# Two-layer trunk on one core: where the end of the first layer splits conv weights, and where the residual is formed

## The chip, the cores and the metric

The kernel runs on one core of a Trainium2 chip: TensorE (matmuls and transposes; in profiles PE, its weight loads PEld), VectorE (DVE), ScalarE (ACT), GpSimd (POOL) and SyncE (SP, which only issues DMAs here). The metric is the device time of one execution in microseconds (us). One run of the profiler gives a trace of one execution; times in it count from its first instruction.

## The reference, cut to what matters

Two layers over 512 latent tokens of width 1024 (the first also reads 256 context tokens). Each layer is a mixer, a post-norm, a mixture of 16 experts and a second post-norm. The change lies where the first layer ends and the second layer's mixer begins.

```python
def _post_norm(h, branch, g, b):
    return _layer_norm(DEEPNORM_ALPHA * h + branch, g, b)

def _short_conv_mixer(u, w_in, conv_w, w_out):              # second layer
    b_gate, c_gate, x_in = jnp.split(u @ w_in, 3, axis=-1)
    z = lax.conv_general_dilated(c_gate * x_in, conv_w[:, None, :], ...)   # depthwise, width 3
    return (b_gate * z) @ w_out

    # in each layer
    u_lat = _modulate(h_lat, m_lat[0], m_lat[1])            # h * (1 + scale) + shift
    y_lat = ...mixer(u_lat, ...)
    h_lat = _post_norm(h_lat, m_lat[2] * y_lat, ln_mix_g[layer], ln_mix_b[layer])
    f_lat = _expert_choice_ffn(_modulate(h_lat, m_lat[3], m_lat[4]), ...)
    h_lat = _post_norm(h_lat, m_lat[5] * f_lat, ln_ffn_g[layer], ln_ffn_b[layer])
```

All data is fp32. Where fp32 accuracy of a projection is needed, both operands are split into a high part (rounded to fp32r) and a low part (the rest), and three matmuls hh + hl + lh are summed.

## The kernel before

**Data.** `A` and `H` are two tiles of 128 x 4 x 1024 (token tile `t` of 4, then the features). In the experts `A` collects the sum of the residual and the experts' outputs, and `H` holds the normed tokens without gain and bias. Gain and bias go into the modulation of the next projection (`NG`) and, separately, into the residual of the next post-norm: alpha * (n * gain + bias).

**The end of the first layer** (`moe`, last expert, e = 15). TensorE transposes the last hidden state (L1380), builds the scatter matrix (L1322), and then makes four rows of 512 that hold the residual's gain and bias on all partitions (`ln_row`: L283 on TensorE, L285 on ScalarE, 16 fp32 matmuls, which the trace shows as 32 passes). Behind them come the last down projection in two column halves (`out_mm`, L1412, from the transfers `wdl`), the scattered sums (L1428) and the norms: for token tiles 0 and 1 VectorE takes the statistics (L1448), the inverse root (L261, L262 on ScalarE; L268 to L273 on VectorE) and writes `H` (L1544).

**Weights of the input projection.** `wci` comes in eight pieces `ci0` to `ci7`, one per block of 128 columns; each holds three sets (C, x and B gate), so set `i` = 3f + b belongs to block f. `prep_conv(i)` splits set `i`: a cast on ScalarE (L247, 128x1024) and a subtraction on GpSimd or VectorE (L248), into one of four slots of a ring. Before the change sets 0 to 2 are split in `open_conv`, ahead of the norms in program order, and set 3 behind the second norm; all four subtractions run on GpSimd.

**The residual** (`residual`, L293 and L294): for each half of a token tile GpSimd multiplies `H` by the gain row and adds the bias row, 128x512 each, into `A`: 16 instructions, eight behind the first two norms and eight behind the last two.

**Then** `post1` makes the projection's input: for each half b of the tokens and each group g of two feature blocks TensorE transposes (L1584), ScalarE modulates (L1588) and casts (L247), VectorE subtracts (L248). `conv_in` is the projection's matmuls (L252 to L254) into `p_c`: the first block's three sums in the banks g, u and d (`p_c_g`, `p_c_u`, `p_c_d`), first for tokens 0 to 255, then for 256 to 511.

**The mixer's loop** (`layer1_mixer`) runs over f = 0 to 7 and b = 0 to 2. Each step is one `conv_in`, the split of set i + 3 (GpSimd; for i = 1 VectorE), one step of the modulation of this layer, and the gate, convolution and product for the block: L1660 on ScalarE, L1662, L1663, L1665 and L1668 on VectorE, then the split of the result for the output projection. The modulation's weights (`wmod`, pieces m1_4 to m1_11) are not multiplied on TensorE: VectorE sums them (L347, L349, eight per piece) into `rows`, and TensorE only adds over the partitions (L407 or L313), at a fixed place in its queue between two blocks. In the last two blocks GpSimd takes a part of these sums (L363, L365).

**What sets the order.** The program order is written out by hand; each engine runs its own instructions in that order and waits at each for what it needs. SP issues the transfers in one queue: a piece of weights is issued when the block that it goes to has been read (`next_load`). So m1_4 goes out when the three sets of `ci0` have been split.

Of the kernel before, what the change touches and what calls it, by code (L numbers as in the profile page):

```python
# [8 lines left out]
F32 = mybir.dt.float32  # L9
F32R = mybir.dt.float32r  # L10
BF16 = mybir.dt.bfloat16
AF = mybir.ActivationFunctionType
ALU = mybir.AluOpType
# [177 lines left out]
class Trunk:  # L191
# [1065 lines left out]
    def moe(self, layer):  # L1257
# [6 lines left out]
        with tc.tile_pool(name=f"ex{layer}", bufs=2) as wk:  # L1264
# [87 lines left out]
            for e in range(NE):  # L1352
                xe = xes[e // 2]
                before = prev

                def scatters(t0):
                    for t in (t0, t0 + 1) if before else ():
                        scatter(*before, t)

                p_g = product("g", lambda k: xe[k // KH][:, k % KH, e % 2], f"g{layer}_{e}", (lambda: scatters(0) if e == NE - 1 else None) if e else lambda: gather(0, 4, KO), e == 0)  # L1360
                sg = wk.tile([P, 512], F32, name="sg", bufs=1)
                nc.scalar.activation(sg, p_g, AF.Silu)
                if e == NE - 1:
                    scatters(2)
                g = e // 2 + 1
                if g < NE // 2 and e % 2 == 0:
                    sel_build(g)
                p_u = product("u", lambda k: xe[k // KH][:, k % KH, e % 2], f"u{layer}_{e}", None, e == 0)
                if e == 0 and self.late:
                    self.late()  # L1370
                hid = self.rows()
                nc.vector.tensor_tensor(hid, sg, p_u, ALU.mult)  # L1372

                if e < NE - 1:
                    scatters(0)
                if g < NE // 2:
                    gather(g, 4 * (e % 2), 4 * (e % 2) + 4, tag="g")
                p_t = self.bank("tr", (P, 4, P), "p_t")
                for q in range(4):
                    nc.tensor.transpose(p_t[:, q], hid[:, q * P:(q + 1) * P], self.cv("ident"))  # L1380
                hT = wk.tile([P, 4, P], F32, name="hT", bufs=1)
                nc.vector.tensor_copy(hT, p_t)
                if e < NE - 1:
                    scatters(2)
                st = scatter_sel(e)
                if self.spare and not gb:
                    gb += [self.spare[:, v * D:v * D + D] for v in range(2)]
                    g1 = [side(v) for v in gb]
                    for v in range(2):
                        self.ln_row(4 * layer + 2 + v, g1[v], 1.0 if last else ALPHA)  # L1390
                lhs = lambda k: hT[:, k % 4, (k // 4) * CAP:(k // 4) * CAP + CAP]
                yp = wk.tile([P, 2, 512], F32R, name="yp", bufs=1)
                if e < NE - 1:
                    split_y(product("d", lhs, f"d{layer}_{e}"), yp, self.m5b)
                    prev = (e, st, yp)
# [81 lines left out]
            for t in range(TT):  # L1477
                if t < 2 - last:
                    part(t, 0)
                else:  # L1480
                    early_sum(t, 0)
            out_mm(1, KH, KO)
            for t in range(2 - last, TT):
                if last:
# [55 lines left out]
            else:  # L1540
# [9 lines left out]
                for t in range(2):  # L1550
                    newton[t]()
                    norm(t)
                self.rs.append(self.prep_conv(3, nc.gpsimd))
                for t in (2, 3):
                    nc.vector.bn_stats(bst[:, t, 0], A[:, t, 0:512])
                total(2)
# [2 lines left out]
                total(3)  # L1559
                for g in range(2, 4):  # L1560
                    self.post1(0, g, wk)
                for t in range(2):
                    self.residual(t, g1)
                rstd(2, 4)()
                for t in (2, 3):
                    norm(t)
# [1 line left out]
                self.p_c = [self.bank(q, name="p_c") for q in "gud"]  # L1568
                self.conv_in(self.p_c[0], self.rs[0], 0, 256)
                self.conv_in(self.p_c[1], self.rs[1], 0, 256)  # L1570
                for g in range(4):
                    self.post1(1, g, wk)
                for t in range(2, TT):
                    self.residual(t, g1)

    def post1(self, b, g, wk):

# [15 lines left out]
    def conv_in(self, out, r, n0, n1):  # L1593
        uH, uL = self.u1
        for k in range(KO):
            self.mm3(out[:, n0:n1], r[:, 0, k], r[:, 1, k], uH[:, k, n0:n1], uL[:, k, n0:n1], k == 0, k == KO - 1)

    def open_conv(self):

        self.rblk, self.ublk = self.freed[-4:-2], self.freed[-2:]  # L1600
        self.ring = [self.block(b, F32R).rearrange("p (i s k c) -> p i s k c", i=2, s=2, k=KO) for b in self.rblk]
        self.rs = [self.prep_conv(i, self.nc.gpsimd) for i in range(3)]
        self.next_load(self.w["ci0"][1])
        self.u1 = [self.block(b, F32R).rearrange("p (k n) -> p k n", k=KO) for b in self.ublk]

    def prep_conv(self, i, eng=None):
# [6 lines left out]
    def layer1_mixer(self):  # L1613
        nc, tc, ins, base = self.nc, self.tc, self.ins, self.base
        uH, uL = self.u1
        with tc.tile_pool(name="l1", bufs=1) as pool:
# [1 line left out]
            gL = pool.tile([P, KO, S], F32R, name="gL")  # L1618
            rx, ry = self.rblk

            hx = base.tile([P, TT, D], F32, tag="H", name="H")
            self.H = hx
            self.load_gates(1, hx[:, 3])
            cbs, zbs = ([hx[:, a, i * 512:i * 512 + 512] for i in range(2)] for a in range(2))
            tb = hx[:, 2, 0:S + 2]
# [16 lines left out]
            for f in range(KO):  # L1642
# [4 lines left out]
                for b in range(3):  # L1647
                    i = 3 * f + b
                    p_b = self.bank(name=f"p_c{b}") if f else p_c[b]
                    self.conv_in(p_b, rs[i], 0 if f else 256, 512)  # L1650
                    if i and i + 3 < 3 * KO:
                        rs.append(self.prep_conv(i + 3, nc.gpsimd if i > 1 else None))
                    elif i + 3 >= 3 * KO:

                        out_rows(i - 1)
# [53 lines left out]
```

## Time and profile before

| | before |
|---|---|
| median of 3 runs | 1477.01 us (1476.96 to 1478.04) |
| the profiled execution | 1474.1 us |
| its span, first to last instruction | 1472.0 us |
| TensorE matmuls, busy | 1370.1 us (93%) |
| VectorE | 708.2 us (48%) |
| ScalarE | 335.9 us (23%) |
| GpSimd | 269.7 us (18%) |

Read it by stages: the first layer's experts run to about 737 us, the norms and the first matmuls of the second layer from there to 790, its input projection to about 924, and the second layer's experts start near 1000. Busy shares over the whole span say little on the stretch from 737 to 924, where the change lies. A row of the timeline gives start, length, engine, line, operation, output<-input, shape, and how often it ran in a row; in brackets stand the engine's idle time before it and what ended that.

### The profile page before, as it was taken

The numbers are of one execution on the slowest core, as the hardware profiler recorded it, in microseconds if no ns is written. First come the engines' busy times: TensorE is split into PE (matmuls) and PEld (weight loads), VectorE is DVE, ScalarE is ACT, GpSimd is POOL, SyncE is SP. The second block draws the span as 40 slices with busy tenths as digits, with TensorE's granted clock in tenths as the row PEclk, the third lists the DMA queues.
The fourth block names the chain that finished last, engine by engine and source line by source line (L and its number), as shares of the span: only waits on it lengthen the run. The fifth ranks groups of instructions, "written<-read, shape, count | busy, mean of one in ns | idle before, by whom it ended". The sixth has DMA issues, their size and how long they took to land. (4 is left out here: it accounts for less than half of the span.)

```text
span 1472.0 us, 17439 instructions
## 1 busy us (share of the span) xinstructions
PE 1370.1 (93%) x7162; PEld 775.1 (53%) x7162; DVE 708.2 (48%) x1158; ACT 335.9 (23%) x661; POOL 269.7 (18%) x239
## 2 busy tenths in 40 slices
PE   7989988889999999999959999989999999999993
PEld 4865546754454444443348787775444454454342
DVE  3684768823243343332476798660333334243246
ACT  2455661321111111011043222231101111111113
POOL 1321628550000000000065445005000000000003
PEclk9989999789999999999979999989999999999996
DMA  9337337789999999999962554749999999999991
GB/s 373 157 130 288 134 136 314 297 322 394 427 426 427 427 427 426 427 426 427 417 277 78 230 229 172 276 180 350 423 427 427 426 426 427 426 427 427 426 407 65
DMA packets 42527, 490.35 MB, mean 333 GB/s; under 512 B 4752, under 2 KB 5200, under 8 KB 13136
## 3 DMA queue, kind: packets, MB, share of 16 engines
q1 hardware_dynamic: 41856, 486.10, 80.1%
q10 hardware_dynamic: 592, 3.15, 0.6%
q8 instruction: 56, 0.92, 0.2%
q14 instruction: 23, 0.19, 0.0%
HBM read 487.13 MB, written 2.10 MB: 332 GB/s over the span
## 5 line engine op out<-in xcount | busy, mean ns | idle before, releaser
L1312 PE MATMUL p_u<-blk,xe 128*64 128x512 f32 x1024 | 226.2, 593 | 6.2 <-DMA blk<-wu 6.2
L1312 PE MATMUL p_g<-blk,xe 128*64 128x512 f32 x1024 | 226.2, 593 | 2.2 <-ACT xe L1299 2.2
L1312 PE MATMUL p_d<-blk,hT 128*64 128x512 f32 x960 | 212.6, 595 | 0.0
L1372 DVE TENSOR_TENSOR rows<-sg,p_u 128x512 f32<-128x512 f32 x32 | 22.0, 688 | 326.1 <-PE p_u L1312 316.0
L1343 DVE SCALAR_TENSOR_TENSOR A<-p_sc_sc,gates,A 128x512 f32<-128x512 f32 x240 | 163.1, 742 | 6.0 <-PE p_sc_sc L1340 6.0
L1312 PEld LDWEIGHTS p_u<-blk,xe 128*64 128x64 f32 x1024 | 72.5, 137 | 154.2 <-issue 140.6
L1312 PEld LDWEIGHTS p_g<-blk,xe 128*64 128x64 f32 x1024 | 72.6, 137 | 146.9 <-issue 139.7
L1402 POOL COPY m5c<-m5b 64x256 f32<-64x256 f32 x8 | 3.2, 394 | 721.9 <-PE p_ga_g L1290 721.6
L1312 PEld LDWEIGHTS p_d<-blk,hT 128*64 128x64 f32 x960 | 66.0, 137 | 129.3 <-issue 129.2
L1299 ACT ACTIVATE xe<-p_ga_g,FG 128x128 f32<-128x128 f32 x112 | 42.1, 455 | 306.5 <-PE p_ga_g L1290 306.5
L1290 PEld LDWEIGHTS p_ga_g<-sel,H 128*128 128x128 f32 x896 | 104.2, 192 | 3.1 <-issue 0.8
L1290 PE MATMUL p_ga_g<-sel,H 128*128 128x128 f32 x896 | 104.7, 275 | 0.0
L1334 ACT CAST yp<-rows 64x512 fp32r<-64x512 f32 (+1 forms) x68 | 40.2, 591 | 270.5 <-DVE rows L1331 269.6
L1331 DVE TENSOR_TENSOR rows<-p_d,m5b 128x512 f32<-128x512 f32 x30 | 20.8, 692 | 134.4 <-PE p_d L1312 134.4
L1340 PE MATMUL p_sc_sc<-yp,st 128*128 128x512 f32 x240 | 72.8, 421 | 1.0 <-DVE A L1343 1.0
L248 POOL TENSOR_TENSOR blk<-blk,blk 128x1024 fp32r<-128x1024 f32 (+1 forms) x25 | 59.8, 2412 | 66.4 <-ACT blk L247 66.4
L252 PE MATMUL p_c_sc<-blk,blk 128*128 128x512 f32 x168 | 67.3, 401 | 0.0
L253 PE MATMUL p_c_sc<-blk,blk 128*128 128x512 f32 x168 | 65.9, 392 | 0.0
L254 PE MATMUL p_c_sc<-blk,blk 128*128 128x512 f32 x168 | 65.8, 392 | 0.0
L1340 PEld LDWEIGHTS p_sc_sc<-yp,st 128*128 128x128 f32 x240 | 40.6, 188 | 34.3 <-issue 24.3
L1335 DVE TENSOR_TENSOR yp<-rows,yp 64x512 fp32r<-64x512 f32 (+1 forms) x68 | 45.6, 671 | 25.3 <-ACT yp L1334 24.2
L349 DVE SCALAR_TENSOR_TENSOR rows<-blk,cond,rows 128x512 f32<-128x512 f32 x49 | 54.2, 1106 | 1.5
(397 smaller groups left out, 2007.7 us busy)
## 6 DMA issues: line engine op xcount, KB each, us to landing
blk<-wg SPq DMA_DIRECT2D x60, 2048.0 KB, 27.8
blk<-wu SPq DMA_DIRECT2D x60, 2048.0 KB, 22.0
blk<-wd SPq DMA_DIRECT2D x56, 2048.0 KB, 26.1
blk<-wmod SPq DMA_DIRECT2D x23, 2048.0 KB, 8.7
blk<-wci SPq DMA_DIRECT2D x8, 1536.0 KB, 12.1
blk<-wd SPq DMA_DIRECT2D x8, 1024.0 KB, 6.7
blk<-wg SPq DMA_DIRECT2D x8, 1024.0 KB, 9.4
blk<-wu SPq DMA_DIRECT2D x16, 512.0 KB, 22.9
```

The lines of the kernel that those rows point to most:

```text
L248: (eng or nc.vector).tensor_tensor(lo, src, hi.bitcast(F32), ALU.subtract)
L252: mm(out, ah, bh, start=start, stop=False)
L253: mm(out, ah, bl, start=False, stop=False)
L254: mm(out, al, bh, start=False, stop=stop)
L349: nc.vector.scalar_tensor_tensor(a, W[:, k], c, a, ALU.mult, ALU.add)
L1290: nc.tensor.matmul(pg[:, j - j0], H[:, t, j * P:(j + 1) * P], sels[g][:, t, e0:e1].rearrange("p e s -> p (e s)"), start=t == 0, stop=t == ...
L1299: nc.scalar.activation(o, pg[:, j - j0], AF.Identity, bias=self.FG[:, 1, j:j + 1], scale=self.FG[:, 0, j:j + 1])
L1312: nc.tensor.matmul(o[64 * hf:64 * hf + 64], lhs(k), W[:, kk, hf * 512:hf * 512 + 512], start=k == 0, stop=k == KO - 1)
L1334: nc.scalar.copy(yp[r, hf], ye[r])
L1335: nc.vector.tensor_tensor(yp[q, hf], ye[r], yp[r, hf].bitcast(F32), ALU.subtract)
L1340: nc.tensor.matmul(pp[hf], st[:, t * P:(t + 1) * P], yp[:, hf], start=True, stop=True)
L1343: nc.vector.scalar_tensor_tensor(a, pp[hf], self.gateT[:, t, e:e + 1], a, ALU.mult, ALU.add)
```

## The change

- The first layer's `ln_row` calls are gone from the last expert. They stand in the mixer's loop at i = 1 (gain) and i = 2 (bias), into tiles of their own (`l1gb`).
- `open_ring` splits set 0 between the two halves of the last down projection's second column half (cast and subtraction on ScalarE and GpSimd). `open_conv` splits set 1 on GpSimd. Set 2 is split by VectorE behind the last norm, and `next_load` of `ci0`'s block stands behind it. Set 3 is split on GpSimd between the groups of the second half's `post1`.
- The residual is formed in place in the tile of the normed tokens, in the mixer's loop at i = 4, 6, ..., 18: one half of a token tile each time (one multiplication, one addition on GpSimd). The mixer's scratch `hx` takes the other tile; the two names `A` and `H` change places.

```diff
@@ moe
-                if self.spare and not gb:
+                if last and self.spare and not gb:
                     gb += [self.spare[:, v * D:v * D + D] for v in range(2)]
                     g1 = [side(v) for v in gb]
                     for v in range(2):
-                        self.ln_row(4 * layer + 2 + v, g1[v], 1.0 if last else ALPHA)
+                        self.ln_row(4 * layer + 2 + v, g1[v], 1.0)
@@ moe, behind the first half of out_mm(1) and the sums of column half 0
+            if not last:
+                self.open_ring()
             out_mm(1, KH, KO)
@@ moe, behind the norms of tiles 0 and 1
-                self.rs.append(self.prep_conv(3, nc.gpsimd))
...
-                for t in range(2):
-                    self.residual(t, g1)
                 rstd(2, 4)()
                 for t in (2, 3):
                     norm(t)
...
                 self.conv_in(self.p_c[0], self.rs[0], 0, 256)
                 self.conv_in(self.p_c[1], self.rs[1], 0, 256)
+                self.rs.append(self.prep_conv(2))
+                self.next_load(self.w["ci0"][1])
                 for g in range(4):
                     self.post1(1, g, wk)
-                for t in range(2, TT):
-                    self.residual(t, g1)
+                    if g == 1:
+                        self.rs.append(self.prep_conv(3, nc.gpsimd))
@@
+    def open_ring(self):
+
+        self.rblk = self.freed[-3:-1]
+        self.ring = [self.block(b, F32R).rearrange("p (i s k c) -> p i s k c", i=2, s=2, k=KO) for b in self.rblk]
+        self.rs = [self.prep_conv(0, self.nc.gpsimd)]
+
     def open_conv(self):
-
-        self.rblk, self.ublk = self.freed[-4:-2], self.freed[-2:]
-        self.ring = [...]
-        self.rs = [self.prep_conv(i, self.nc.gpsimd) for i in range(3)]
-        self.next_load(self.w["ci0"][1])
+        assert self.rblk == self.freed[-4:-2]
+        self.ublk = self.freed[-2:]
+        self.rs.append(self.prep_conv(1, self.nc.gpsimd))
@@ layer1_mixer
-            hx = base.tile([P, TT, D], F32, tag="H", name="H")
-            self.H = hx
+            hx = base.tile([P, TT, D], F32, tag="A", name="A")
+            self.H, self.A = hx, self.H
+            gb = [[pool.tile([P, 512], F32, name=f"l1gb{v}{h}") for h in range(2)] for v in range(2)]
+
+            def residual(q):
+                a = self.A[:, q // 2, (q % 2) * 512:(q % 2) * 512 + 512]
+                nc.gpsimd.tensor_tensor(a, a, gb[0][q % 2], ALU.mult)
+                nc.gpsimd.tensor_tensor(a, a, gb[1][q % 2], ALU.add)
+
...
                     self.conv_in(p_b, rs[i], 0 if f else 256, 512)
+                    if i in (1, 2):
+                        self.ln_row(1 + i, gb[i - 1], ALPHA)
+                    if i in range(4, 20, 2):
+                        residual(i // 2 - 2)
                     if i and i + 3 < 3 * KO:
                         rs.append(self.prep_conv(i + 3, nc.gpsimd if i > 1 else None))
```

What stands in the engines' queues, first TensorE at the end of the last expert, before (-) against now (`p_gb` are the gain and bias rows, `p_d` and `p_u` the two column halves of the down projection):

```order
 L1322 LDWEIGHTS identb
 L1322 MATMUL p_sb_tr<-slotb,identb 128x512
-L283 MATMUL p_gb_sc<-lnr,cst 128x128 x16
 L1412 MATMUL p_d<-blk_124_4248,hT 64x256 x16
 L1412 MATMUL p_u<-blk_125_4261,hT 64x256 x8
```

The 16 matmuls of the rows no longer stand ahead of the down projection. Next GpSimd from the early sums (L1423) on, before (`blk_126` is `ci0`, `blk_127` is `ci1`, `blk_130` the gain and bias rows):

```order
L1423 TENSOR_TENSOR A<-A,l_y 128x512 x2
L248 TENSOR_TENSOR blk_131_4531<-blk_126_4277,blk_131_4531 128x1024 x2
L248 TENSOR_TENSOR blk_132_4532<-blk_126_4277,blk_132_4532 128x1024
L248 TENSOR_TENSOR blk_132_4532<-blk_127_4287,blk_132_4532 128x1024
L293 TENSOR_TENSOR A<-H,blk_130_4414 128x512
L294 TENSOR_TENSOR A<-A,blk_130_4414 128x512
```

and now (L1632 and L1633 are the residual, `l1gb` its rows; `blk_128` is `ci2`):

```order
L1423 TENSOR_TENSOR A<-A,l_y 128x512 x2
L248 TENSOR_TENSOR blk_131_4493<-blk_126_4277,blk_131_4493 128x1024 x2
L248 TENSOR_TENSOR blk_132_4494<-blk_127_4287,blk_132_4494 128x1024
L1638 MEMSET A 128x1
L1639 MEMSET A 128x1
L248 TENSOR_TENSOR blk_131_4493<-blk_127_4287,blk_131_4493 128x1024
L248 TENSOR_TENSOR blk_132_4494<-blk_128_4336,blk_132_4494 128x1024
L1632 TENSOR_TENSOR H<-H,l1gb_4717 128x512
L1633 TENSOR_TENSOR H<-H,l1gb_4719 128x512
```

Sets 0 and 1 stand directly behind the early sums, set 3 behind them, and the first pair of the residual behind the splits of sets 5 and 6; before, the residual's eight pairs stood between set 3 and set 5. Last ScalarE at the start of the mixer's loop, before:

```order
L1660 COPY H<-p_c_g 128x512
L247 CAST blk_131_4531<-blk_127_4287 128x1024 x2
L247 CAST gH<-H 128x512
L247 CAST blk_132_4532<-blk_128_4336 128x1024
L1660 COPY H<-p_c_sc 128x512
```

and now:

```order
L1676 COPY A<-p_c_g 128x512
L285 ACTIVATE l1gb_4717<-p_gb_sc 128x512
L285 ACTIVATE l1gb_4718<-p_gb_sc 128x512
L247 CAST blk_131_4493<-blk_127_4287 128x1024
L285 ACTIVATE l1gb_4719<-p_gb_sc 128x512
L285 ACTIVATE l1gb_4720<-p_gb_sc 128x512
L247 CAST blk_131_4493<-blk_127_4287 128x1024
L247 CAST gH<-A 128x512
```

Two copies of the gain rows stand ahead of the cast of set 4, and two of the bias rows ahead of that of set 5.

## Rows read from the trace of the kernel before

**Rows 1.** Windows: busy us (count) of PE, PEld, DVE, ACT, POOL; clock; DMA.
```profile
753.00:766.00 13.00, 1.34 (x5) 1.05 (x6) 12.62 (x19) 2.61 (x6) 12.29 (x7) 0.53 0.59 231
840.00:908.00 68.00, 68.00 (x312) 56.34 (x310) 62.04 (x62) 15.73 (x19) 37.57 (x17) 1.00 0.56 222
```
**Rows 2.** Timeline of TensorE at the last expert's end: start, us, what, [idle before].
```profile
737.00 3.83 PE L283 MATMUL p_gb_sc<-lnr,cst 64*128 64x128 f32 x32
740.77 3.67 PE L1412 MATMUL p_d<-blk,hT 128*64 128x256 f32 x32
...
747.46 1.95 PE L1412 MATMUL p_u<-blk,hT 128*64 128x256 f32 x16
```
**Rows 3.** SP's issues there, and us from issue to landing (last number).
```profile
723.92 9.24 SPq L215 DMA_DIRECT2D blk<-wdl  x8
...
734.16 0.33 SPq L215 DMA_DIRECT2D blk<-wci  x1
...
blk<-wdl SPq DMA_DIRECT2D x1, 512.0 KB, 10.2
...
blk<-wci SPq DMA_DIRECT2D x1, 1536.0 KB, 12.6
```
**Rows 4.** Timeline of ScalarE: the cast of the second column half.
```profile
750.07 0.83 ACT L1334 CAST yp<-rows 64x256 fp32r<-64x256 f32 x2 [1.47 <-DVE rows L1331]
```
**Rows 5.** Timeline of GpSimd and VectorE around the norms.
```profile
752.05 9.25 POOL L248 TENSOR_TENSOR blk<-blk,blk 128x1024 fp32r<-128x1024 f32 x4 [1.40 <-ACT blk L247]
...
755.63 1.09 DVE L268 SCALAR_TENSOR_TENSOR rs_t<-l_r 128x1 f32<-128x1 f32 x1
...
761.77 0.21 DVE L268 SCALAR_TENSOR_TENSOR rs_t<-l_r 128x1 f32<-128x1 f32 x1
...
763.24 1.84 DVE L1544 TENSOR_SCALAR H<-A,l_nm,l_r 128x1024 f32<-128x1024 f32 x1
...
775.38 1.54 DVE L1544 TENSOR_SCALAR H<-A,l_nm,l_r 128x1024 f32<-128x1024 f32 x2
```
**Rows 6.** Timeline of VectorE: the subtractions of the projection's input.
```profile
768.24 2.79 DVE L248 TENSOR_TENSOR blk<-u1t,blk 128x512 fp32r<-128x512 f32 x2
...
782.25 6.65 DVE L248 TENSOR_TENSOR blk<-u1t,blk 128x512 fp32r<-128x512 f32 x4 [5.34 <-ACT blk L247]
```
**Rows 7.** Timeline of ScalarE and VectorE at the start of the mixer's loop.
```profile
789.85 0.59 ACT L1660 COPY H<-p_c_g 128x512 f32<-128x512 f32 x1 [2.92 <-PE p_c_g L254]
790.33 1.05 ACT L247 CAST blk<-blk 128x1024 fp32r<-128x1024 f32 x1
792.61 1.05 ACT L247 CAST blk<-blk 128x1024 fp32r<-128x1024 f32 x1 [1.23 <-PE p_c_u L253]
...
791.47 1.23 DVE L248 TENSOR_TENSOR blk<-blk,blk 128x1024 fp32r<-128x1024 f32 x1 [2.57 <-ACT blk L247]
...
807.37 0.69 DVE L409 TENSOR_TENSOR H<-mod_b_sc,H 128x512 f32<-128x512 f32 x1 [1.94 <-PE mod_b_sc L407]
```
**Rows 8.** Timeline of VectorE without and with GpSimd beside it; then that window.
```profile
850.71 1.54 DVE L1665 SCALAR_TENSOR_TENSOR H<-H,vec 128x512 f32<-128x512 f32 x2
852.16 3.11 DVE L349 SCALAR_TENSOR_TENSOR rows<-blk,cond,rows 128x512 f32<-128x512 f32 x4
...
900.89 2.85 DVE L1665 SCALAR_TENSOR_TENSOR H<-H,vec 128x512 f32<-128x512 f32 x2
903.67 6.37 DVE L349 SCALAR_TENSOR_TENSOR rows<-blk,cond,rows 128x512 f32<-128x512 f32 x4
...
901.76:909.96 8.20, 6.31 (x28) 4.88 (x26) 8.06 (x6) 0.00 (x0) 7.97 (x6) 1.00 0.00 0
```
**Rows 9.** Timeline of VectorE: what it waits for in the projection.
```profile
829.03 1.57 DVE L347 TENSOR_SCALAR rows<-blk,cond 128x512 f32<-128x512 f32 x1 [6.19 <-DMA blk<-wmod]
...
874.35 0.16 DVE L318 TENSOR_TENSOR mlat<-mod_pc_sc,vec 128x4 f32<-128x4 f32 x1 [1.10 <-PE mod_pc_sc L313]
...
891.62 0.16 DVE L318 TENSOR_TENSOR mlat<-mod_pc_sc,vec 128x4 f32<-128x4 f32 x1 [1.46 <-PE mod_pc_sc L313]
```

More of the change, by code (lines that the diff above doesn't have):

```diff
@@ L1596, in conv_in @@
             self.mm3(out[:, n0:n1], r[:, 0, k], r[:, 1, k], uH[:, k, n0:n1], uL[:, k, n0:n1], k == 0, k == KO - 1)
+    def open_ring(self):
+        self.rblk = self.freed[-3:-1]
+        self.ring = [self.block(b, F32R).rearrange("p (i s k c) -> p i s k c", i=2, s=2, k=KO) for b in self.rblk]
+        self.rs = [self.prep_conv(0, self.nc.gpsimd)]
     def open_conv(self):
-        self.rblk, self.ublk = self.freed[-4:-2], self.freed[-2:]
-        self.ring = [self.block(b, F32R).rearrange("p (i s k c) -> p i s k c", i=2, s=2, k=KO) for b in self.rblk]
-        self.rs = [self.prep_conv(i, self.nc.gpsimd) for i in range(3)]
-        self.next_load(self.w["ci0"][1])
+        assert self.rblk == self.freed[-4:-2]
+        self.ublk = self.freed[-2:]
+        self.rs.append(self.prep_conv(1, self.nc.gpsimd))
         self.u1 = [self.block(b, F32R).rearrange("p (k n) -> p k n", k=KO) for b in self.ublk]
```

## The prediction

> **What bounds the kernel now.** I read the windows by stage first. Between 753 and 766 us TensorE works 1.34 us of 13 at a granted clock of 0.53, while VectorE and GpSimd are both busy for over 12 us; between 840 and 908 us TensorE is busy all 68 us, VectorE 62 and GpSimd 37.6 [rows 1]. So the change touches two stages with different limits. At the end of the first layer TensorE waits for VectorE's norms. In the input projection of the second layer TensorE is the bound, but with VectorE right behind it. Next I read the waits there: between 840 and 908 us VectorE waits for TensorE only twice, 1.10 and 1.46 us, and before that once for a weight transfer, 6.19 us [rows 9]. That is all the room it has for delay.
>
> The third view is the timeline of VectorE beside that of GpSimd, and it gives the price on which everything turns. Six VectorE instructions (two L1665, four L349) take 1.54 + 3.11 = 4.65 us when GpSimd stands still. The same six took 2.85 + 6.37 = 9.22 us beside GpSimd's short multiplies and adds: six of those and six of VectorE's share the window from 901.76 to 909.96, GpSimd busy for 7.97 us of it [rows 8]. That is 0.76 us lost for each GpSimd instruction: the two engines take turns, each waiting for the other's instruction to end. The second price comes from the residual itself: four L248 took 6.65 us beside four of its instructions [rows 6], against 4 x 0.78 = 3.11 at the pace of the free L349, so 0.88 us each.
>
> **Part by part, on the way to the end of p_c_g (the first block of the input projection).**
> 1. The four rows of gain and bias leave TensorE's queue ahead of the last expert's output. L283 took 3.83 us from 737.00 and L1412 began at 740.77 without a wait [rows 2]. Its weights are there earlier: eight parts were issued from 723.92 on, and each lands 10.2 us later, the first at 734.1, the last (issued 8.9 us after it) at 743.0 [rows 3]. The matmuls that read the last two began at 747.46 [rows 2], now at 743.7, and come to the last part near 744.6. So the whole is won: **-3.8**.
> 2. ScalarE's cast for ring block 0 now stands ahead of the second L1334. It waits for ci0, issued at 734.16 and landed 12.6 us later, at 746.8 [rows 3], and takes 1.05 us [rows 7], to 747.8. L1334 began at 750.07 [rows 4] and could begin at 746.3. So **+1.5**.
> 3. VectorE's stretch from 755.63 to the end of the second norm at 765.08 took 9.45 us while GpSimd split four sets from 752.05 to 761.30 without a break [rows 5]. Free of that it holds two norms (1.54) and six tiny instructions, of which the unhindered one took 0.21 [rows 5]: about 2.8 us. GpSimd's two early splits (9.25 / 4 = 2.3 us each) run from 747.8 to 752.5, and the stretch now begins near 753.4, so they are over: **-6.7**.
> 4. The first two L248 took 2.79 us beside the residual [rows 6], against 1.56 free: **-1.2**. The next two gain less, since ScalarE's pace feeds them; I count them as nothing.
> 5. In the second half the four L248 lose their neighbours too, but ScalarE gets a further cast (1.05 us) between them and sets the pace: **-0.5**, bounds 0 and -1.5. Split 2 on VectorE stands beside TensorE's projection of p_c_g and p_c_u, which hides it; the transfer that it releases (m1_4, next in SP's queue) is issued some 9 us later than before, and is needed only at VectorE's first L347, behind the split of step 6.
> Together -10.7 at the end of p_c_g: ScalarE's copy moves from 789.85 [rows 7] to about 779.1. TensorE's granted clock was 0.53 between 753 and 766 us [rows 1], nearly all at the lower of its two levels (1.2 GHz), after it had waited for the norms; I keep that. If it stayed at 2.4 GHz, some 4 us of matmuls there would take half: 2 us more won (an estimate), as bound.
>
> **In the input projection.**
> 6. ScalarE's cast for ring block 4 began at 790.33, half a us after the copy, and VectorE's split of it at 791.47 [rows 7]. Now two copies of the gain stand ahead of it on ScalarE, and those wait for half of L283, which waits for p_c_u (done at 792.61, 2.8 us after the copy began). So 2.8 + 1.9 + 0.6 (a copy of that size, row 789.85) puts the cast at 784.4 and VectorE's split at 785.6: of 10.7 us, 5.9 are left on VectorE. TensorE pays all of L283 again, 3.8 us, in a stretch that has no idle time; the bias matmul that VectorE's L409 waited for (807.37, after a wait of 1.94 [rows 7]) comes 10.7 - 3.8 = 6.9 us earlier, and VectorE is there by then. **Won at that place: 6.9 us.** With nothing else the change would end there: 1467.2 in the profiled execution.
> 7. The residual: 16 GpSimd instructions of 128x512 between the splits of column blocks 1 to 6. Before, they stood in the stage of the norms (part of what steps 3 to 5 win back); now they stand beside VectorE's sums and convolution, which have two operands in SBUF. I take 0.88, since it is the price of these very instructions: 16 x 0.88 = 14.1 us. From it go the two waits for TensorE (1.10 + 1.46) and about 0.9 for an instruction of residual 2 that runs inside the wait of 6.19 us: 10.6 us on VectorE. TensorE's bias and column matmuls (L407, L313) wait for VectorE's sums in its own queue, so each us that VectorE falls behind stops TensorE. **+10.6.** Lower bound: VectorE is idle 6 of the 68 us [rows 1], and L1662 and L1668 read PSUM; about an eighth of the instructions would fall beside those, so 0.76 x 7/8 = 0.66, or 10.6 - 3.5 = 7.1. Upper bound: VectorE loses the whole of each instruction, 1.33 us (7.97 / 6 [rows 8]): 21.3 - 3.5 = 17.8.
>
> What the rows show of this (0.76 and 0.88 lost for instructions of about 1.3 us) bears on a rule of the Trainium skill, "SBUF — State Buffer", section "Who interferes with whom": a VectorE instruction with two SBUF inputs contends with a GpSimd instruction that reads SBUF, and the one that starts first holds the shared ports for its whole length. By the rule the loss may be the whole 1.33 us each, which would give +10.9 instead of +3.7, and 1487.9; the rows lie below it because VectorE often asks when part of the GpSimd instruction is already over.
>
> **Sum.** -6.9 + 10.6 = +3.7 us. The profiled execution took 1474.1 us (span 1472.0); the median of the runs is 1477.01, 2.9 above it. So 1477.8 in a profiled execution and 1480.7 as a median. Behind the projection every weight load is released by the projection's own instructions, so I let the shift through to the end unchanged.
>
> **Rivals.**
> A. *The residual hides.* GpSimd stood idle for 30 of the 68 us between 840 and 908 [rows 1]; if its short instructions met only VectorE instructions that read PSUM or wait, the 6.9 us would stay: 1470.1. It decides at a price of (6.9 + 3.5) / 16 = 0.65 us for even, and of 0.46 for a gain of 0.2%. Against it: VectorE's 62 of 68 us [rows 1] and both measured prices. Half of the residuals stand ahead of a split whose cast is done, not in the idle stretch.
> B. *Even.* VectorE's price comes out near 0.65, because the splits behind the residual move into stretches in which VectorE waits: 1474.1 to 1479.9, say 1477.
> C. *The early splits still run beside the norms.* If ci0 or ScalarE's two casts come 2 us later than I count, split 1 (2.3 us) blocks L268 as it did at 755.63 (1.09 us [rows 5]) and TensorE idles on: 3.7 + 2.3, or 1483.0. That is the case in which the change does not do what it says.
>
> **How the numbers follow.** A difference of under 0.2% (2.95 us) can't be told from no change here. Forecast 0.60, and a sixth of it lies within 0.2%; A 0.13; B 0.20; C 0.07. Faster: A and a tenth of B, 0.15. Same: 0.10 of the forecast and 0.18 of B, 0.28. Slower: 0.50 + 0.07 = 0.57. Range: the sum runs from -6.9 + 7.1 = +0.2 to +10.9, and the clock adds 2 at the lower end: 1475 to 1488. The upper end needs the worst price for all sixteen, so I stop at 1486.5, which with A leaves out under 2 in 10.
>
> **What would show it.** Step 1: L1412 directly behind L1322, near 737.0. Step 2: ScalarE idle until 746.8 ahead of the first L247. Step 3: the second norm ends near 756 us, none of the six tiny instructions over 0.3 us. Steps 4 and 5: the copy L1676 near 779. Step 6: VectorE idle for over 5 us ahead of a split that begins near 785.6. Step 7: L1681 and L349 of 1.4 to 1.8 us beside L1632 and L1633, and TensorE waits ahead of L407 and L313 that sum to some 7 to 10 us more than before. I am wrong if TensorE is as dense between 800 and 900 us as before; then the price of the residual is what failed. If the copy of step 5 stands at 783 or later, the early gain failed.

## The result, and the profile after

The changed kernel takes 1484.78 us (median of 4 runs, 1483.59 to 1485.99) against 1476.99 before: ratio 1.0056, 95% interval 1.0040 to 1.0072; by the medians it is 7.8 us slower. The prediction was 1480.7, 3.7 slower: the right side, inside its range, and half the size. Its profiled execution took 1485.99 us.

Executions start the stretch at slightly different times, so traces are compared here from L1322, the scatter matrix ahead of the last down projection: 736.70 before, 735.58 after. "Earlier" and "later" below are counted from it.

TensorE's timeline after (start, us, what, [idle before]):

```profile
735.58 0.38 PE L1322 MATMUL p_sb_tr<-slotb,identb 128*128 128x512 bf16 x1 [0.78 <-DVE hT L1382]
735.88 3.67 PE L1412 MATMUL p_d<-blk,hT 128*64 128x256 f32 x32
...
749.61 0.55 PE L1428 MATMUL p_sc_sc<-yp,st 128*128 128x256 f32 x1 [5.10 <-DVE yp L1335]
752.00 1.44 PE L1428 MATMUL p_sc_sc<-yp,st 128*128 128x256 f32 x5 [1.84 <-DVE yp L1335]
757.88 0.48 PE L1585 MATMUL p_tr_sc<-cst,H 128*128 128x128 f32 x1 [4.45 <-DVE H L1546]
...
934.08 0.50 PE L252 MATMUL p_y_sc<-blk,gH 128*128 128x512 f32 x1
```

L1412 stands directly behind L1322: the rows are gone from there. But TensorE now waits 5.10 and 1.84 us for the split of the hidden rows (L1335), where before it was 1.68; its first wait for the norms is 4.45 us instead of 9.62. The last line is the first matmul of the output projection, p_y; before:

```profile
736.70 0.38 PE L1322 MATMUL p_sb_tr<-slotb,identb 128*128 128x512 bf16 x1 [0.78 <-DVE hT L1382]
...
751.08 1.21 PE L1428 MATMUL p_sc_sc<-yp,st 128*128 128x256 f32 x6 [1.68 <-DVE yp L1335]
761.91 0.47 PE L1584 MATMUL p_tr_sc<-cst,H 128*128 128x128 f32 x1 [9.62 <-DVE H L1544]
...
924.85 0.50 PE L252 MATMUL p_y_sc<-blk,gH 128*128 128x512 f32 x1
```

From L1322 to p_y it is 188.15 us before and 198.50 after: 10.4 later. VectorE and GpSimd after, the two timelines behind those first waits:

```profile
747.10 4.85 DVE L1335 TENSOR_TENSOR yp<-rows,yp 64x256 fp32r<-64x256 f32 x2 [1.95 <-ACT yp L1334]
...
758.38 0.81 DVE L1546 TENSOR_SCALAR H<-A,l_nm,l_r 128x1024 f32<-128x1024 f32 x1
...
746.83 4.83 POOL L248 TENSOR_TENSOR blk<-blk,blk 128x1024 fp32r<-128x1024 f32 x2 [1.08 <-ACT blk L247]
```

The two early splits run from 746.83 to 751.66, and two small subtractions of VectorE, which take 0.87 us without a neighbour (the first line of e3 below), end 0.3 us behind them. The second norm (758.38) is done 4.8 us earlier than in [rows 5], not 9. ScalarE and VectorE after, at the start of the loop:

```profile
780.63 0.58 ACT L1676 COPY A<-p_c_g 128x512 f32<-128x512 f32 x1 [1.68 <-PE p_c_g L254]
784.59 0.60 ACT L285 ACTIVATE l1gb<-p_gb_sc 128x512 f32<-128x512 f32 x1 [3.38 <-PE p_gb_sc L283]
785.48 0.60 ACT L285 ACTIVATE l1gb<-p_gb_sc 128x512 f32<-128x512 f32 x1 [0.30 <-PE p_gb_sc L283]
785.98 1.04 ACT L247 CAST blk<-blk 128x1024 fp32r<-128x1024 f32 x1
...
787.05 1.22 DVE L248 TENSOR_TENSOR blk<-blk,blk 128x1024 fp32r<-128x1024 f32 x1 [7.37 <-ACT blk L247]
```

The copy of p_c_g is 8.1 us earlier than in [rows 7], the split of set 4 only 3.3, after a wait of 7.37 us. From there VectorE falls behind. TensorE's waits in the loop (in all, times, longest), before:

```profile
PE mod_b_sc L412 <- DVE rows L349: 2.1, 1, 2.1
PE mod_b_sc L407 <- DVE rows L349: 2.1, 1, 2.1
PE mod_pc_sc L313 <- DVE rows L349: 0.9, 1, 0.9
```

and after:

```profile
PE mod_b_sc L407 <- DVE rows L349: 6.2, 1, 6.2
PE mod_b_sc L412 <- DVE rows L349: 5.0, 1, 5.0
PE mod_pc_sc L313 <- DVE rows L349: 4.9, 3, 2.3
```

The windows from the first bias matmul (m4) to p_y (columns as in [rows 1]), before, with the stretch behind the wait of 2.07 us under it:

```profile
806.31:924.85 118.54, 113.42 (x498) 90.77 (x496) 100.75 (x111) 26.81 (x36) 55.55 (x28) 0.99 0.53 210
820.32:838.74 18.42, 17.48 (x74) 13.82 (x75) 11.22 (x16) 4.06 (x5) 7.15 (x3) 1.00 0.58 229
```

and after, with the stretch behind the wait of 6.15 us:

```profile
801.48:934.08 132.60, 116.56 (x497) 92.00 (x495) 117.90 (x111) 26.93 (x37) 81.83 (x44) 0.95 0.48 190
819.57:824.00 4.43, 4.43 (x8) 2.82 (x9) 1.93 (x3) 2.99 (x4) 2.21 (x1) 0.50 0.86 281
```

That stage grew by 14.06 us. 10.92 of it is idle time of TensorE (16.04 against 5.12). The other 3.14 is TensorE's own time for the same matmuls: the granted clock over the stage fell from 0.99 to 0.95. Directly behind the wait of 6.15 us it is 0.50, the lower level (1.2 GHz), for 4.43 us; behind the wait of 2.07 us before it was 1.00.

### The profile page after: what moved, and what is told of

Read it like the earlier page. It is cut to its first block, busy times and chain, and to the rows that moved or that the text cites. A ratio compares the mean times of both kernels' runs of the same rounds, so it can differ in the third digit from the quotient of the medians.

```text
span 1484.1 us, 17438 instructions
## 1 busy us (share of the span) xinstructions
PE 1375.2 (93%) x7162; PEld 777.5 (52%) x7162; DVE 718.7 (48%) x1159; ACT 335.7 (23%) x661; POOL 270.7 (18%) x238
## 4 chain that ended last, share of the span: by engine, by line
PE 62%; DMA 17%; DVE 16%; ACT 2%; issue 2%; DVEq 0%; SPq 0%; ACTq 0%
PE p_g L1312 11%; PE p_d L1312 11%; PE p_u L1312 10%; DMA blk<-wg 5%; DMA blk<-wu 5%; DMA blk<-wd 5%; PE p_ga_g L1290 5%; DVE rows L349 3%; PE p_sc_sc L1340 3%; PE p_y_sc L252 2%; PE p_y_sc L254 2%; PE p_y_sc L253 2%; DVE A L1681 1%; PE mod_R L306 1%; PE p_o L931 1%
## 5 line engine op out<-in xcount | busy, mean ns | idle before, releaser
L1334 ACT CAST yp<-rows 64x512 fp32r<-64x512 f32 (+1 forms) x68 | 40.2, 591 | 279.3 <-DVE rows L1331 278.5
L1343 DVE SCALAR_TENSOR_TENSOR A<-p_sc_sc,gates,A 128x512 f32<-128x512 f32 x120 | 81.6, 743 | 3.0 <-PE p_sc_sc L1340 3.0
L1343 DVE SCALAR_TENSOR_TENSOR H<-p_sc_sc,gates,H 128x512 f32<-128x512 f32 x120 | 81.6, 743 | 3.0 <-PE p_sc_sc L1340 3.0
L248 POOL TENSOR_TENSOR blk<-blk,blk 128x1024 fp32r<-128x1024 f32 (+1 forms) x24 | 59.4, 2487 | 79.8 <-ACT blk L247 79.8
L1335 DVE TENSOR_TENSOR yp<-rows,yp 64x512 fp32r<-64x512 f32 (+1 forms) x68 | 49.6, 730 | 27.0 <-ACT yp L1334 26.0
L349 DVE SCALAR_TENSOR_TENSOR rows<-blk,cond,rows 128x512 f32<-128x512 f32 x49 | 61.5, 1255 | 1.5
L1362 ACT ACTIVATE sg<-p_g 128x512 f32<-128x512 f32 x32 | 19.1, 597 | 154.3 <-PE p_g L1312 154.3
```

The lines of the kernel that those rows point to most:

```text
L248: (eng or nc.vector).tensor_tensor(lo, src, hi.bitcast(F32), ALU.subtract)
L349: nc.vector.scalar_tensor_tensor(a, W[:, k], c, a, ALU.mult, ALU.add)
L1334: nc.scalar.copy(yp[r, hf], ye[r])
L1335: nc.vector.tensor_tensor(yp[q, hf], ye[r], yp[r, hf].bitcast(F32), ALU.subtract)
L1343: nc.vector.scalar_tensor_tensor(a, pp[hf], self.gateT[:, t, e:e + 1], a, ALU.mult, ALU.add)
```

## The experiments

Ratios are to the kernel before, run beside it on the same chip; differences in us between runs are worked out from them, unless a median is named. Each interval reaches 2 to 3 us to either side, so a difference of that size between two runs rests on the traces. "At p_y" is the place of p_y in the trace, counted from L1322, against before. Sums of VectorE's durations in the expectations count the small overlap of neighbours; the windows shown here don't, and read some 3 us less.

### The changed kernel again (e9)

> The changed kernel once more, unaltered, beside the two others of this call: a second trace of it and more runs. Ratio to before 1.004 to 1.0072 if the first comparison holds. The first trace lay 10.4 us behind the one of before at the first matmul of the output projection, while the medians differ by 7.8; if the first trace is typical, this one shows 9.5 to 11 at the same place, counted from the scatter matrix of the last expert (L1322).

Ratio 1.0054 (1.0035 to 1.0073); at p_y 11.3 us later, just above what was expected. So both traces lie 10.4 to 11.3 behind, and both comparisons of medians give 7.7 to 7.8. The loop repeats (m4 to p_y 132.70 us, against 132.60 in the first trace); the copy of p_c_g is 7.2 us earlier than before, against 8.1. The executions differ from one another where nothing was changed, too: L1322 stands anywhere from 734.3 to 737.7 us in the traces of this study. What makes up the 3 us between traces and medians was not found; the kernel before has one trace only, of an execution 2.9 us below its median.

### The residual left out (e1)

```diff
-                    if i in range(4, 20, 2):
-                        residual(i // 2 - 2)
```

> The 16 instructions of the residual on GpSimd are left out (what the second layer's post-norm adds is then the normed tile without gain and bias); their rows are still made. In the changed kernel VectorE's instructions between its split of set 4 and the bias matmul of m10 took 45.6 us longer than the shortest of their kind, in the kernel before 27.4. Only 13.2 of the 45.6 stand beside the residual itself; the splits' share grew too, 22.5 to 27.2. Theory 1 (the residual is the cause, both by its own turns and by pushing the splits into stretches where VectorE is dense): the excess falls to 25 to 30 us, TensorE's waits ahead of the bias and column matmuls from 16 us to about 5, and the time to 1471 to 1475 (ratio to before 0.996 to 0.9985). Theory 2 (only the 13.2 us of direct turns matter): excess near 32, time 1475 to 1479. Rival (the rows in the mixer's loop and the late start of set 4's cast set the time): above 1481.

Ratio 0.9966 (0.9952 to 0.9980): 5 us faster than before, 13 less than the changed kernel; at p_y 3.1 us earlier. The windows from the copy of p_c_g to the bias matmul of m10, after and then e1:

```profile
780.63:918.96 138.33, 122.30 (x572) 100.15 (x571) 118.68 (x108) 29.06 (x37) 84.45 (x45) 0.97 0.43 171
```

```profile
781.58:906.63 125.05, 119.60 (x572) 99.06 (x571) 101.70 (x108) 29.28 (x37) 56.42 (x26) 1.00 0.48 189
802.42:921.31 118.89, 113.44 (x498) 90.87 (x496) 101.13 (x111) 27.15 (x37) 55.81 (x28) 0.99 0.54 211
```

VectorE runs the same 108 instructions in 101.70 us instead of 118.68: the 16 instructions cost it 16.98 us, 1.06 each. In the second line (m4 to p_y, as above) TensorE idles for 5.45 us and is busy for 113.44: both the waits and the clock are as before. So the residual in the loop is the whole loss of that stage; without it the lower clock is gone too. The excess over the shortest of each kind came to 27.7 us, as theory 1 put it. VectorE's waits in that window (in all, times, longest), after and then e1:

```profile
DVE rows L347 <- DMA blk<-wmod: 4.8, 1, 4.8
DVE A L409 <- PE mod_b_sc L407: 1.8, 2, 1.6
```

```profile
DVE rows L347 <- DMA blk<-wmod: 6.1, 1, 6.1
DVE mlat L318 <- PE mod_pc_sc L313: 2.6, 2, 1.5
DVE A L409 <- PE mod_b_sc L407: 1.6, 1, 1.6
```

After, the two waits for L313 are gone and the wait for the weights is 1.3 us shorter; the waits for ScalarE are the same in both.

### The residual behind the split (e8)

```diff
-                    if i in range(4, 20, 2):
-                        residual(i // 2 - 2)
                     if i and i + 3 < 3 * KO:
...
+                    if i in range(4, 20, 2):
+                        residual(i // 2 - 2)
```

> The changed kernel with one order exchanged on GpSimd: each pair of the residual stands behind the split of its step, not ahead of it. Nothing is left out. VectorE was busy for 121.7 us between the copy of p_c_g and m10 in the changed kernel, 104.6 without the residual: 17.1 more, of which 13.2 stand directly beside the residual. Theory (the rest, some 4 us, comes from splits pushed into stretches where VectorE is dense): the splits return to the times they had without a residual, VectorE's busy time falls to 116 to 119, the time by 2 to 5 us, to a ratio of 1.002 to 1.0045. Rival (only the number of turns counts, wherever they fall): ratio 1.0045 to 1.007, as the changed kernel.

Ratio 1.0058 (1.0043 to 1.0072): the rival. The window of e8, copy of p_c_g to m10:

```profile
781.22:920.88 139.66, 124.56 (x572) 102.11 (x571) 119.19 (x108) 29.06 (x37) 83.28 (x45) 0.95 0.43 169
```

119.19 us against 118.68: this exchange on GpSimd changes nothing. That part of theory 1 (splits pushed into dense stretches) falls. Which of GpSimd's instructions stood beside VectorE's said little here about which one cost the time.

### The residual on VectorE (e4)

```diff
-                nc.gpsimd.tensor_tensor(a, a, gb[0][q % 2], ALU.mult)
-                nc.gpsimd.tensor_tensor(a, a, gb[1][q % 2], ALU.add)
+                nc.vector.tensor_tensor(a, a, gb[0][q % 2], ALU.mult)
+                nc.vector.tensor_tensor(a, a, gb[1][q % 2], ALU.add)
```

> The 16 residual instructions run on VectorE at the same places, nothing else is changed. Each should take 0.69 us there, 11.0 us in all, as added work of the engine that is behind. Theory 1 (on GpSimd they cost VectorE more than twice that: 13.2 us of turns and about 9 us more through the displaced splits): the time falls by 6 to 10 us, to 1475 to 1479. Theory 2 (only the direct turns count, 13.2 against 11.0): by 1 to 3 us, to 1482 to 1484. Rival (VectorE's own length is what matters, and GpSimd's turns are partly hidden in its waits): 1485 to 1490.

Ratio 1.0040 (1.0022 to 1.0057), 2.4 us less than the changed kernel, as theory 2, though the two intervals overlap; at p_y 7.0 later, against 10.4 and 11.3. But not for its reason. VectorE's groups by line in the loop (busy us, mean ns):

```profile
L1633 DVE TENSOR_TENSOR H<-H,l1gb 128x512 f32<-128x512 f32 x8 | 18.0, 2249 | 0.3
L1632 DVE TENSOR_TENSOR H<-H,l1gb 128x512 f32<-128x512 f32 x8 | 5.5, 683 | 0.0
```

The eight multiplications took 683 ns each, the eight additions behind them 2249, because by then one of GpSimd's splits runs. The 16 took 23.5 us of VectorE, not 11.0, and it was busy no less than with GpSimd doing them (119.67 against 118.68 us). Part of that fell into its wait for the next modulation weights, which is 1.82 us here and 4.83 in the changed kernel.

### The residual's place on ScalarE (e11)

```diff
-                nc.gpsimd.tensor_tensor(a, a, gb[0][q % 2], ALU.mult)
-                nc.gpsimd.tensor_tensor(a, a, gb[1][q % 2], ALU.add)
+                nc.scalar.activation(a, a, AF.Copy, scale=ALPHA)
+                nc.scalar.activation(a, a, AF.Copy, scale=1.0)
```

> The changed kernel with each of the 16 residual instructions replaced by a copy of the same 128x512 piece in place on ScalarE, at the same places of the program; gain and bias are left out, so the residual's values are others (the rows are made all the same). Theory (the loss is a matter of VectorE and GpSimd alone, which take turns): VectorE's instructions in the loop keep the length they have without a residual, 104 to 106 us busy between the copy of p_c_g and m10, and the ratio is 0.996 to 0.999. Rival (any third engine that reads and writes this much slows VectorE): VectorE busy above 112 us, ratio above 1.002.

Ratio 0.999 (0.997 to 1.001); at p_y 0.6 us earlier. Its window, copy of p_c_g to m10:

```profile
781.63:909.45 127.82, 120.99 (x573) 100.23 (x571) 104.55 (x108) 38.42 (x53) 58.70 (x29) 0.99 0.47 184
```

VectorE's 108 instructions take 104.55 us: 2.85 more than without a residual, against 16.98 more with it on GpSimd. By far the most of the loss is between VectorE and GpSimd. (The copies read one operand each and the residual's instructions two; what that makes of the difference was not tested.) Why the time is at the slow end of what was expected stays open.

### The rows left out (e2)

```diff
+            for v in range(4):
+                nc.gpsimd.memset(gb[v // 2][v % 2], 1.0)
...
-                    if i in (1, 2):
-                        self.ln_row(1 + i, gb[i - 1], ALPHA)
```

> The rows of gain and bias are left out: the four tiles are set to 1.0 by GpSimd ahead of the mixer's loop, so the residual adds other values; everything else is the changed kernel. Theory (the rows cost their 3.8 us on TensorE and hold ScalarE's cast of set 4 back by 4 to 5 us, and all that VectorE does behind it): VectorE's split of set 4 begins 4 to 5 us earlier after the copy of p_c_g, and the time falls by 4 to 5 us to 1480 to 1481. Rival (the lag of VectorE behind the residual swallows it, or the transfer of the next modulation weights lands no earlier): within 1.5 us of the changed kernel, 1483 to 1486.

Ratio 1.0024 (1.0010 to 1.0037): 4.7 us less than the changed kernel, as the theory said; at p_y 3.4 us less. VectorE of e2 at set 4, 1.56 us behind the copy of p_c_g (779.99) instead of 6.42:

```profile
781.55 1.23 DVE L248 TENSOR_TENSOR blk<-blk,blk 128x1024 fp32r<-128x1024 f32 x1 [2.52 <-ACT blk L247]
```

### The cast behind the down projection (e3)

```diff
+            out_mm(1, KH, KO)
             if not last:
                 self.open_ring()
-            out_mm(1, KH, KO)
...
-        self.rblk = self.freed[-3:-1]
+        self.rblk = self.freed[-4:-2]
```

> Ring block 0 is split behind the second half of the last down projection, so ScalarE's two casts of the hidden rows (L1334) stand ahead of the cast of set 0. In the changed kernel VectorE's two subtractions L1335 took 4.85 us from 747.10 beside GpSimd's two splits (4.83 us from 746.83), where 0.87 would do, and TensorE waited 5.10 and 1.84 us for them. Theory (the early splits only moved onto these two instructions): L1335 takes about 0.9 us and ends near 747, the second norm ends 4 to 5 us earlier, and the time falls by 3 to 4.5 us, to 1480 to 1482. Rival (the two splits then stand beside the norms' short instructions again and take it back): second norm within 1.5 us, time 1483.5 to 1486.

Ratio 1.0032 (1.0017 to 1.0048): 3.5 us less than the changed kernel. VectorE and GpSimd of e3:

```profile
747.86 0.87 DVE L1335 TENSOR_TENSOR yp<-rows,yp 64x256 fp32r<-64x256 f32 x2 [0.47 <-ACT yp L1334]
...
752.98 1.10 DVE L268 SCALAR_TENSOR_TENSOR rs_t<-l_r 128x1 f32<-128x1 f32 x1
...
749.40 4.65 POOL L248 TENSOR_TENSOR blk<-blk,blk 128x1024 fp32r<-128x1024 f32 x2 [1.40 <-PE p_sc_sc L1428]
```

L1335 takes 0.87 us, and behind it the splits run beside sums that read PSUM (L1435) and statistics (L1448), which take 0.75 and 0.69 us as without a split beside them. Only one short instruction of the norms, L268, still meets a split: 1.10 us instead of 0.21. The second norm comes 7.9 us earlier than before and the copy of p_c_g 11.2, against 4.8 and 8.1 in the changed kernel: 3.1 us more, where 4 to 5 were expected at the norm.

### The splits' move alone (e10, e12)

The kernel before, with this, and without its splits of sets 2 and 3 at their old places (e12 has set 3's split behind both halves of the residual):

```diff
+            if not last:
+                self.open_ring()
             out_mm(1, KH, KO)
...
-                self.rs.append(self.prep_conv(3, nc.gpsimd))
...
+                self.rs.append(self.prep_conv(2))
+                self.next_load(self.w["ci0"][1])
                 for g in range(4):
                     self.post1(1, g, wk)
+                    if g == 1:
+                        self.rs.append(self.prep_conv(3, nc.gpsimd))
```

> The kernel before with only the new order of the splits of sets 0 to 3; the rows are again made in the last expert ahead of the down projection, and GpSimd forms the residual behind the norms. Nothing is left out. Theory (the splits' move gains by itself what the norms lost beside them, less what the two subtractions L1335 lose, and the loop is as before): second norm 2 to 4 us earlier than in the kernel before, the copy of p_c_g 2 to 5 us earlier, all of it kept: ratio 0.9965 to 0.999. Rival (the residual then runs beside what the splits left free, and only its move made the early gain): copy within 1 us of before, ratio 0.999 to 1.002.

> As e10_splits_only, with set 3's split behind both halves of the residual in GpSimd's queue. In e10 that split waited for ScalarE's cast at 781.71 between the two halves, the residual ended at 796.4 and ScalarE's copy of p_c_g, which writes into the tile that the residual reads, waited 10.80 us for it. Theory (only that queue position spoiled e10; its second norm was 2.8 us early): the residual ends ahead of the last L248, the copy of p_c_g comes 2 to 4 us earlier than in the kernel before, and the ratio is 0.997 to 0.9995. Rival (the residual's first half starts earlier but its second waits for the norms as before, and set 3 is now late for the loop): ratio 0.9995 to 1.003.

e10: ratio 1.0044 (1.0028 to 1.0060), neither theory nor rival. The second norm came 2.8 us earlier, but the copy of p_c_g 5.9 later. GpSimd and ScalarE of e10:

```profile
782.83 2.38 POOL L248 TENSOR_TENSOR blk<-blk,blk 128x1024 fp32r<-128x1024 f32 x1 [11.08 <-ACT blk L247]
...
795.15 1.29 POOL L294 TENSOR_TENSOR A<-A,blk 128x512 f32<-128x512 f32 x1
...
796.69 0.59 ACT L1669 COPY H<-p_c_g 128x512 f32<-128x512 f32 x1 [10.80 <-POOL H L1636]
```

GpSimd stood for 11.08 us at set 3's split, which waits for ScalarE, with half of the residual queued behind it; the copy then waited 10.80 us for the residual to leave the tile that it writes (L1636, which the line names, is a small write to that tile behind the residual in GpSimd's queue). With the split behind the residual (e12) the residual ends at 787.9, the copy is 3.0 us earlier than before, and the ratio is 0.9978 (0.9964 to 0.9992). So the splits alone gain 3 us, and the residual may stay where it was.

### Other places for the residual and the rows (e5 to e7)

e5 takes the residual out of the loop and into `mix_out`: the half tiles (0, 0) and (1, 0) on GpSimd ahead of the first sum, the other six on VectorE behind the sums of `evac`. e6 adds the diff shown here, e7 that of e3 as well.

```diff
-                    if i in (1, 2):
-                        self.ln_row(1 + i, gb[i - 1], ALPHA)
+                    if i in (6, 21):
+                        v = int(i > 6)
+                        self.ln_row(2 + v, gb[v], ALPHA, ("d", "tr") if v else ("g", "u"))
```

> The residual leaves the mixer's loop for the output projection behind it, where VectorE waits 2.2 to 4.3 us for TensorE between the sums of two token tiles: two half tiles on GpSimd ahead of the first sum, six on VectorE in those waits. Nothing is left out. Theory (its cost in the loop was contention with an engine without slack; here there is slack): the time of the run without a residual, ratio to before 0.996 to 0.998. Rival (it costs the same wherever VectorE works, since the sums it delays stand ahead of the second layer's experts): ratio above 1.000.

> As e5_residual_at_sums, and the rows of gain and bias are made behind blocks 6 and 21 of the loop, where TensorE waits for VectorE's sums of the modulation (2.42 and 2.12 us in the run without a residual), into PSUM banks that the loop doesn't use. Theory (TensorE's 3.8 us then lie in its waits, and ScalarE's cast of set 4 no longer waits for the rows): 3 to 4 us less than e5, ratio 0.9935 to 0.9955. Rival (the waits move with VectorE, which is as early as its own transfers allow): within 1.5 us of e5, ratio 0.996 to 0.9975.

> As e6_rows_in_waits, and the cast of ring block 0 stands behind the second half of the last down projection, as in e3_cast_behind. Theory (the three effects add): 2.5 to 3.5 us less than e6, ratio 0.991 to 0.994. Rival (with nothing else late, the wait of 6 us for the modulation's weights behind m5 takes the early gain): the ratio of e6.

Ratios 0.9961 (0.9946 to 0.9976), 0.9941 (0.9924 to 0.9959) and 0.9906 (0.9889 to 0.9923). At p_y they are 2.5, 7.0 and 10.1 us earlier than before; e1, with no residual at all, was 3.1. The new place lies behind p_y, so its cost is read from there to a copy of the experts' gating that stands behind all of the residual (L1347, in e5 L1355); e1 and then e5:

```profile
921.31 0.50 PE L252 MATMUL p_y_sc<-blk,gH 128*128 128x512 f32 x1
...
990.90 0.19 POOL L1347 COPY smc<-sel 128x1 f32<-128x1 f32 x1 [20.88 <-DVE sel L1278]
```

```profile
922.57 0.50 PE L252 MATMUL p_y_sc<-blk,gH 128*128 128x512 f32 x1
...
992.16 0.19 POOL L1355 COPY smc<-sel 128x1 f32<-128x1 f32 x1 [20.88 <-DVE sel L1286]
```

It is 69.59 us in both: the residual costs nothing in its new place, where in the loop it cost 13.4 at p_y. From the copy of p_c_g to p_y e6 needs 1.1 us more than the kernel before, so little of the rows' cost is left. From e6 to e7 the traces gain 3.1 us, as expected; e7's ratio lies just below the range expected. e7 takes 1461.58 us, 14 less than the kernel before beside it. Its window (copy of p_c_g to m10) and two of the residual's instructions in VectorE's timeline:

```profile
779.26:901.25 121.99, 120.77 (x573) 100.07 (x571) 102.41 (x108) 28.10 (x35) 55.70 (x26) 0.99 0.49 193
```

```profile
941.34 0.68 DVE L1640 TENSOR_TENSOR H<-H,l1gb 128x512 f32<-128x512 f32 x1
942.05 0.69 DVE L1641 TENSOR_TENSOR H<-H,l1gb 128x512 f32<-128x512 f32 x1
...
945.68 0.69 DVE L1081 TENSOR_TENSOR blk<-p_y_sc,A 128x512 f32<-128x512 f32 x1 [1.61 <-PE p_y_sc L254]
```

TensorE is idle for 1.22 of 121.99 us. On VectorE the residual's instructions take their bare 0.68 and 0.69 us, and it still waits 1.61 us for the next sum.

## Why the prediction came out at half the size

The working put the kernel 10.7 us ahead at the copy of p_c_g, 6.9 ahead at m4 and 3.7 behind at p_y. The first trace shows 8.1 and 3.7 ahead, and 10.4 behind. Step by step:

- **Step 1 (rows out of the last expert) held.** L1412 stands directly behind L1322.
- **Step 2 (the cast waits for `ci0`) had the right wait and missed its consequence.** The cast began at 745.71, about when it was put. But I priced only the cast ahead of L1334, and not the subtraction that the cast releases on GpSimd, which starts just before VectorE's L1335 is ready and holds it for 4 us. At the second norm 4.2 of the 9.0 us of steps 1 to 3 are lost. e3 shows it: with the cast behind, the norm comes 3.1 us earlier, and the copy is 11.2 us early, close to the 10.7 of the sum. The text had the collision as rival C, but against L268, and it came one instruction group earlier.
- **Step 3 (norms freed of the splits) held,** once the splits were over: all six short instructions took 0.15 to 0.21 us. **Steps 4 and 5** were sized 1.7; from second norm to copy the trace gained 3.3. TensorE's granted clock was 0.86 from 760 to 770 us and 1.00 from 770 to 780, against 0.50 and 0.79 before: the bound that the text named, and about its size, though no run has the clock alone.
- **Step 6 (the rows in the loop) held.** From the copy to m4 TensorE needed 20.85 us instead of 16.46, 4.4 more where 3.8 was counted; VectorE waited 7.37 us for set 4, and its lead fell by 4.8 us (8.1 to 3.3), as in the sum (10.7 to 5.9). e2 prices the whole at 4.7.
- **Step 7 (the residual's contention) is the term that was mis-sized:** 10.6 predicted, 14.1 measured. The mechanism held: VectorE falls behind, and TensorE waits for its sums. So did what VectorE's own waits take up: from the copy to m10 its idle time is 23.35 us in e1 and 19.65 after, 3.7 less, where 3.5 was counted. The price did not hold. Each of the 16 instructions cost VectorE 1.06 us, between the 0.88 taken and the bound of 1.33: 17.0 us and not 14.1, which is 2.9 of the 3.5 us missed. Most of that was in the reading of [rows 6]: the free pace taken there, 0.78, is that of L349, while two L248 with GpSimd idle take 1.34, so 0.67 each (the first line below, after). With it the row gives (6.65 - 4 x 0.67) / 4 = 0.99 us. 17.0 less 3.7 is 13.3, just what this window grew by against e1 (138.33 us against 125.05).

TensorE shows these 13.3 us as 10.6 of waits and 2.7 of its own time at the lower clock. That its waits alone (10.9 from m4 to p_y) came out near the 10.6 of the sum is luck. Nor is the clock a second loss here, up to m10. VectorE waited for TensorE 1.8 us in this window, against 4.2 in e1, so TensorE's slower stretches did not hold it up; and m10's bias matmul (second line) came when VectorE's sums were there:

```profile
765.95 1.34 DVE L248 TENSOR_TENSOR blk<-u1t,blk 128x512 fp32r<-128x512 f32 x2
...
918.96 1.94 PE L412 MATMUL mod_b_sc<-rows,cst 128*64 128x512 f32 x2 [4.99 <-DVE rows L349]
```

TensorE stood ready 4.99 us before that, so its time at the lower clock only shortened its waits. From m10 to p_y the kernel after needs 15.12 us and e1 14.68: 0.4 us is what the clock can have added there.

2.6 us at the copy (4.2 lost to the early splits, 1.6 won back by steps 4 and 5), 0.6 from the rows and 3.5 from step 7 make the 6.7 us between 3.7 and the trace's 10.4. Rival A (the residual hides) fell clearly. The rule of the Trainium skill, "SBUF — State Buffer", section "Who interferes with whom", that the whole length of the other instruction may be lost, is the 1.33; the measured price lies between it and the row. The same section of the Trainium skill has VectorE share its second pair of ports with GpSimd alone; e11 agrees, up to the 2.85 us that it shows.

## What to carry to other kernels

Work that looks free because GpSimd idles can cost most of its length when VectorE has no room (1.06 us for each instruction of some 1.3 here): look for a stage in which VectorE waits, and put it there (13.4 us in the projection, nothing beside the sums). When an instruction is moved ahead in one queue, follow what it releases on the next engine and what that meets, not only what it delays. And take a delay from the account of the engine that is waited for: TensorE's waits and its time at the lower clock were two parts of one delay here, and adding the clock to VectorE's loss would have counted it twice.

## What was not expected of the hardware

- Exchanging a split and a pair of the residual in GpSimd's order left VectorE's loss unchanged (119.19 against 118.68 us), though a count by which instruction stood beside which had put nearly a quarter of it on the order.
- Moving the work from GpSimd to VectorE saved little: an addition of 0.69 us took 2.25 on average beside a running split.
- A wait of 6.15 us of TensorE was followed by 4.43 us at half clock; one of 2.07 us in the kernel before by none. Up to m10 the half clock cost nothing more, since TensorE had to wait for VectorE again.
